# Output projection of a four-layer mixer trunk: weight blocks turned from 1024 rows by 256 columns to 512 by 512, with 512 columns per matmul

## Chip, core and metric

The kernel runs on one core of one Trainium2 chip. The metric is the device time of one execution in microseconds; a comparison uses the median of several. A difference below about 0.3% is treated as none.

## The reference

A sequence of 512 latent and 256 context tokens of width 1024 passes through four layers. Each layer normalises its input, scales and shifts it (a modulation computed from a conditioning vector), mixes the tokens, projects the mixed features back to width 1024 and adds the result to the residual stream:

```
h  = rmsnorm(x, g_pre[i]) * (1 + scale) + shift
y  = mixer(h, ...)                # the mixer's last step is: o @ w_out
x  = x + gate * rmsnorm(y, g_post[i])
```

The mixers are gated linear attention (layers 0 and 3), windowed attention (layer 1) and an RG-LRU recurrence (layer 2). `w_out` has 1024 rows in layers 0, 1 and 3 and 1280 rows in layer 2. In the last layer only the 512 latent tokens are projected.

## The kernel before, in words

**Products.** All large products are done in float32 precision by three passes: each operand is split into a high and a low float32r part, and `hi*hi + hi*lo + lo*hi` is accumulated in PSUM. So each chunk of 128 contraction rows costs three matmuls. Activations are held as `Rh` and `Rl`, features on the partitions, in 8 chunks of 128 features by 768 tokens.

**Weights.** `plan` (line 287) lists a layer's weight blocks in the order of use. A block has 1024 rows by 256 columns. `loadw` (line 221) loads it in two DMAs of 512 rows (512 KB each, tile `raw`, two buffers) on the SP queue; its `convert` splits each piece with `split` (line 242): ScalarE writes the high part (line 243), then VectorE, or for every third split GpSimd, writes the low part (line 246). The tiles `wh` and `wl` have two buffers each. `weights` (line 335) hands out the next block and first fetches and converts the one after it, so the conversion of a block waits until the block two before it has been read for the last time.

**The finish of a layer** (`finish`, line 733) opens six PSUM banks of 512 columns. It splits the mixer's output `OG` into `Rh` and `Rl` chunk by chunk (lines 750 and 751), finishes the modulation work that is still pending (`background`, line 753), loads the residual `x`, and then does the output projection for six token tiles of 128 tokens (four in the last layer), context tiles 4 and 5 first:

- Blocks o0 and o1 (the first two quarters of the columns): for each pair of token tiles one bank holds two results of 256 columns; `product` (line 761) issues 24 matmuls of 256 columns for a token tile (30 in layer 2, whose last two contraction chunks come from the tiles `exh`, `exl` and the weights `wxh`, `wxl`). `take` (line 773) then evacuates: ScalarE squares and sums (line 776), VectorE multiplies by the gate row `gpt` (line 777).
- Blocks o2 and o3 (the other two quarters) are both there before `halves` (line 811) runs: for each token tile it does the third quarter, later the fourth, into the two halves of one bank; after the fourth come `take` on 512 columns, `post` (line 781: sum of the three partial sums, then 1/rms on GpSimd, lines 589 and 590) and later `residual` (line 789).
- In layers 0 to 2 the second part is written out by hand (line 864 on; the order on TensorE, ScalarE and VectorE is the program's order). Between the products of `halves` it places what leads to the next layer's operand: `residual`, `square` (line 596), `scale` (line 796, y), then `norm` (transposes at line 613, ScalarE at 617, VectorE at 624 and 625) in four steps for each pair of tiles. In layers 0 and 1 each `step` also carries two matmul groups of a later layer's modulation (line 499, weights `rawp`, with transposes at line 517). The order around the first transposes is:

```
run(halves((2, 4), (2, 5), (3, 4), (3, 5)))
h = halves((2, 0), (2, 1), (3, 0), (3, 1))
...
next(h)            # quarter 2 of tile 0
...
next(h)            # quarter 2 of tile 1
scale(5)
step((4, 5), 0)    # transposes of tiles 4 and 5
```

- In the last layer (`final`, line 824) each token tile runs `halves((2, tt), (3, tt))` and then `residual`, in an order that the planner of the framework may still change by readiness.

After the last product, `begin` (line 401) and the next mixer's first products follow.

Of the kernel before, what the change touches and what calls it, by code (L numbers as in the profile page):

```python
# [10 lines left out]
F32 = mybir.dt.float32  # L11
# [8 lines left out]
P = 128  # L20
# [55 lines left out]
def body(ctx: ExitStack, tc: tile.TileContext, I, out, layers=(0, 1, 2, 3)):  # L76
# [28 lines left out]
    @contextmanager  # L105
    def phase(name, single=2, double=2):
        """a phase's own SBUF pool and the PSUM banks that phases share out anew, singly and in pairs"""
        with ExitStack() as st:
            if open_already:
                st.push(open_already.pop())  # L110
            else:
                open_banks(st, name, single, double)
            yield open_pool(st, name, bufs=1)

# [10 lines left out]
    # the first phase's banks are there from the start  # L125
# [26 lines left out]
    # the RG-LRU's small parameters  # L152
# [7 lines left out]
    def lru_parameters(bank):  # L160
# [10 lines left out]
        # half biases for the gates' tanh form of the sigmoid  # L171
        V.tensor_scalar(hb, ps[:, 50:90], 0.5, None, op0=ALU.mult)
        # softplus(-lam) = max(-lam, 0) + ln(1 + exp(-|lam|)), times -4 and 2
# [13 lines left out]
    class Mixed:  # L187
        """the mixer's output, features on the partitions; its last two chunks' room is free for
        other use until they are written"""
# [31 lines left out]
    def loadw(pieces):  # L221
        """256 columns; what is returned takes them apart once they are there"""
# [18 lines left out]

    def split(h, l, x):
# [5 lines left out]
    def load_g1(a):  # L248
        """the low-rank gate projection, both directions, four times over along the columns"""
# [19 lines left out]
    def load_g2(a, zero=True, load=True):  # L269
        """three times over, each direction's rows against its own columns; gpt is free for it"""  # L270
# [16 lines left out]
    def plan(i):  # L287
        """the layer's weight blocks in the order of use"""
# [31 lines left out]
        for n in range(4):  # L320
            yield f"o{n}", cols(wo[0 : KC * P], (n * 256, 256))
# [13 lines left out]
    def weights(key, ahead=True):  # L335
        """the next weight block, with the one after it on its way"""
# [7 lines left out]
    def passes(ps, a, b, kc):  # L344
        """ps += a^T b for pairs (hi, lo) of operand getters over the contraction chunks."""
# [8 lines left out]
    # products begun ahead of their use: the bank's part, and how many tokens of it are done  # L354
    begun = {}

    def ws_part(w, c0, ps, t0, n):
        """128 output columns on the partitions, tokens along the free axis"""
# [8 lines left out]
    def product_steps(ps, w, c0, t0, n):  # L367
        """the same, one product at a time; yields what each takes"""
# [9 lines left out]
    def ws(w, c0, stream):  # L378
        """128 output columns for all tokens of the stream"""
# [8 lines left out]
    def ws_ctx(w):  # L388
        """the context's tokens for both halves of the columns, in one bank but for what was begun elsewhere"""
# [11 lines left out]
    def begin(stream):  # L401
        """the first 256 tokens of what the next weight block brings first"""
# [11 lines left out]
    def ts(wk, kc, rk, tts, ps=None):  # L414
        """tokens on the partitions, 256 output columns along the free axis, for two token tiles."""
# [15 lines left out]
    def gate(pool, w, c0, stream, dst, parts=1):  # L431
        """dst (128 channels, the stream's tokens) *= silu(z), z a 128-column block of the projection."""
# [3 lines left out]
    def gate_ctx(pool, w, dst):  # L436
        """the same for both of the block's halves"""
        silu_times(pool, ws_ctx(w)[0], dst[:, :, CTX0:])
# [15 lines left out]
    def z_steps(pool, w, c, b, put, streams=("ctx", "lat")):  # L454
        """silu(z) for chunk b of the mixer's output, ahead of the output or behind it; put holds
        the token tiles of which either is there"""
# [48 lines left out]
    def mod_ss(i, n, bank, pool=None, bufs=1):  # L505
        """shift (n 0-3) and scale (n 4-7) of layer i, with the features on the partitions; in three steps."""
# [28 lines left out]
    def mod_gate(i, n, bank, pool=None, bufs=1):  # L535
        """gate * g_post of layer i, on all partitions; in three steps."""
# [34 lines left out]
    def background(n):  # L571
        """the next of the modulations; the last step of each comes with the one after it"""
# [20 lines left out]
    def unit_rstd(pool, x, xn):  # L593
        """1 / rms(x); xn is overwritten"""
# [4 lines left out]
    def unit(pool, x, xn):  # L599
        """xn = x / rms(x)"""  # L600
# [3 lines left out]
    def norm_part(pool, i, pr, xn, k, h=None):  # L604
        """xn: token tile -> x / rms(x); writes two chunks of h of layer i, transposed and split, to Rh / Rl."""
# [21 lines left out]
    def first_norm(i):  # L627
        """the same before the first layer, where the modulation comes late: x / rms(x) waits
        transposed in OG, and goes on as its chunks' shift and scale come in. A GLA's first
        products follow chunk by chunk."""  # L630
# [54 lines left out]
        # (two groups share a bank: the first one's first product clears the flags of both)  # L685
# [47 lines left out]
    def finish(i, kc, extra, last, final, xsrc, xdst):  # L733
        """out projection of OG, post norm, residual, and the next layer's pre norm."""
# [3 lines left out]
        with phase(f"fin{i}", 6, 0) as fp:  # L738
# [15 lines left out]
            for tt in tts_all:  # L754
# [3 lines left out]
                ssq[tt] = fp.tile([P, 3], F32, name=f"ssq{tt}")  # L758
            R = (Rh, Rl)

            def product(w, q, tt, ps, k0=0, k1=kc):
                """a quarter of the columns for a token tile"""
                cq = slice(q * 256, (q + 1) * 256)
                for k in range(k0, k1):
                    for u, v in ((0, 0), (0, 1), (1, 0)):
                        l = R[u][:, k, :] if k < KC else extra[u][:, k - KC, :]
                        r = w[v][:, k, :] if k < KC else wx[v][:, k - KC, cq]
# [5 lines left out]
            def take(q, tt, ps):  # L773
# [918 lines left out]
```

## Time and profile before

| | |
|---|---|
| times of three runs | 1570.82, 1573.35, 1574.89 us (median 1573.35) |
| span of the profiled execution, first to last instruction | 1568.0 us |
| time of the profiled execution itself | not listed; the three times above are 2.8 to 6.9 us over its span |
| TensorE busy with matmuls | 1489.2 us, 95% of the span |
| VectorE, ScalarE, GpSimd busy | 66%, 49%, 18% |
| matmuls | 12819 |
| mean granted TensorE clock | 0.988 of full speed |

The profile names an instruction by its line, its engine and `output<-inputs`. A matmul's listed duration is its passage through the array; since matmuls are pipelined, what counts is the distance between the starts of two neighbours, called pitch below. An idle time in brackets stands in front of the instruction that ended it, with what released it.

### The profile page before, as it was taken

The numbers are of one execution on the slowest core, as the hardware profiler recorded it, in microseconds if no ns is written. First come the engines' busy times: TensorE is split into PE (matmuls) and PEld (weight loads), VectorE is DVE, ScalarE is ACT, GpSimd is POOL, SyncE is SP. The second block draws the span as 40 slices with busy tenths as digits, with TensorE's granted clock in tenths as the row PEclk, the third lists the DMA queues.
The fourth block names the chain that finished last, engine by engine and source line by source line (L and its number), as shares of the span: only waits on it lengthen the run. The fifth ranks groups of instructions, "written<-read, shape, count | busy, mean of one in ns | idle before, by whom it ended". The sixth has DMA issues, their size and how long they took to land.

```text
span 1568.0 us, 31484 instructions
## 1 busy us (share of the span) xinstructions
PE 1489.2 (95%) x12819; PEld 1279.1 (82%) x12819; DVE 1040.6 (66%) x1918; ACT 774.9 (49%) x1567; POOL 289.1 (18%) x338
## 2 busy tenths in 40 slices
PE   6989999999999999999999999899999999999998
PEld 3777788889987777788789877778899877878888
DVE  5586647575363388787872679989852675776753
ACT  5644343534252376565552556666742545454241
POOL 2221302112121200101001212222311311211211
PEclk8999999999999999999999999999999999999999
DMA  9432324113474532222134633222151243112132
GB/s 306 139 114 78 122 62 132 55 47 130 158 235 133 165 83 58 61 59 55 54 115 143 224 102 114 67 64 61 57 176 44 99 143 98 38 53 68 45 108 81
DMA packets 153057, 162.51 MB, mean 104 GB/s; under 512 B 12418, under 2 KB 141968, under 8 KB 152912
## 3 DMA queue, kind: packets, MB, share of 16 engines
q1 hardware_dynamic: 147456, 146.56, 30.6%
q10 hardware_dynamic: 5456, 13.94, 2.5%
q8 instruction: 101, 1.65, 0.4%
q14 instruction: 44, 0.36, 0.1%
HBM read 138.44 MB, written 11.53 MB: 96 GB/s over the span
## 4 chain that ended last, share of the span: by engine, by line
PE 49%; DVE 12%; ACT 5%; issue 4%; DMA 3%; POOL 1%; SPq 1%; POOLq 0%; ACTq 0%; DVEq 0%
PE mxt L768 16%; PE pjt L372 9%; PE pjt L362 5%; PE pjt L349 3%; PE mxt L1464 3%; PE mxt L1450 2%; PE mxt L499 2%; PE sct L1563 2%; DMA raw<-in_w_mod_dram 1%; PE mxt L1146 1%; PE mxt L1412 1%; PE mxt L1395 1%; DVE wl L246 1%; ACT wh L243 1%; DMA bb<-in_b_mod_dram 1%
## 5 line engine op out<-in xcount | busy, mean ns | idle before, releaser
L362 PE MATMUL pjt<-Rh,wh 128*128 128x256 f32 (+1 forms) x592 | 199.6, 338 | 8.8 <-DVE Rh L624 5.3
L768 PE MATMUL mxt<-wh,Rh 128*128 128x256 f32 x704 | 200.7, 285 | 0.0
L362 PE MATMUL pjt<-Rl,wh 128*128 128x256 f32 (+1 forms) x592 | 198.8, 336 | 1.9 <-DVE Rl L625 1.6
L768 PE MATMUL mxt<-wh,Rl 128*128 128x256 f32 x704 | 198.9, 283 | 0.0
L768 PE MATMUL mxt<-wl,Rh 128*128 128x256 f32 x704 | 198.9, 283 | 0.0
L362 PE MATMUL pjt<-Rh,wl 128*128 128x256 f32 (+1 forms) x592 | 197.5, 334 | 0.0
L243 ACT CAST wh<-raw 128x1024 fp32r<-128x1024 f32 x118 | 122.8, 1050 | 88.6 <-PE pjt L362 22.4
L372 PE MATMUL pjt<-Rl,wh 128*128 128x512 f32 (+1 forms) x448 | 161.1, 360 | 0.0
L372 PE MATMUL pjt<-Rh,wh 128*128 128x512 f32 (+1 forms) x448 | 160.4, 358 | 0.0
L372 PE MATMUL pjt<-Rh,wl 128*128 128x512 f32 (+1 forms) x448 | 159.0, 355 | 0.0
L246 POOL TENSOR_TENSOR wl<-raw,wh 128x1024 fp32r<-128x1024 f32 x32 | 85.5, 2670 | 304.0 <-ACT wh L243 232.6
L768 PEld LDWEIGHTS mxt<-wh,Rh 128*128 128x128 f32 x704 | 134.9, 192 | 1.9 <-issue 1.6
L768 PEld LDWEIGHTS mxt<-wh,Rl 128*128 128x128 f32 x704 | 134.7, 192 | 0.3 <-DVE Rl L751 0.2
L768 PEld LDWEIGHTS mxt<-wl,Rh 128*128 128x128 f32 x704 | 134.9, 192 | 0.1
L362 PEld LDWEIGHTS pjt<-Rh,wh 128*128 128x128 f32 x592 | 112.7, 191 | 24.5 <-DVE Rh L624 6.9
L246 DVE TENSOR_TENSOR wl<-raw,wh 128x1024 fp32r<-128x1024 f32 x86 | 110.4, 1289 | 33.1 <-ACT wh L243 32.8
L362 PEld LDWEIGHTS pjt<-Rl,wh 128*128 128x128 f32 x592 | 112.7, 191 | 16.4 <-DVE Rl L625 4.0
L349 PE MATMUL pjt<-wh,Rh 128*128 128x256 f32 x432 | 124.2, 287 | 0.0
L349 PE MATMUL pjt<-wl,Rh 128*128 128x256 f32 x432 | 123.9, 287 | 0.0
L349 PE MATMUL pjt<-wh,Rl 128*128 128x256 f32 x432 | 123.8, 286 | 0.0
L362 PEld LDWEIGHTS pjt<-Rh,wl 128*128 128x128 f32 x592 | 112.9, 191 | 13.0 <-issue 1.2
L777 DVE TENSOR_TENSOR y<-mxt,gpt 128x256 f32<-128x256 f32 (+1 forms) x66 | 33.6, 512 | 110.8 <-ACT y L776 110.8
(293 smaller groups left out, 3673.9 us busy)
## 6 DMA issues: line engine op xcount, KB each, us to landing
rawp<-in_w_mod_dram SPq DMA_DIRECT2D x48, 512.0 KB, 6.2
raw<-in_w_mod_dram SPq DMA_DIRECT2D x48, 512.0 KB, 3.6
raw<-in_a_w_in_dram SPq DMA_DIRECT2D x32, 512.0 KB, 3.5
raw<-in_b_w_in_dram SPq DMA_DIRECT2D x20, 512.0 KB, 4.6
raw<-in_c_w_in_dram SPq DMA_DIRECT2D x20, 512.0 KB, 3.6
xd<-x SPq DMA_DIRECT2D x18, 512.0 KB, 2.6
raw<-in_a_w_out_dram SPq DMA_DIRECT2D x16, 512.0 KB, 3.4
x<-xd ACTq DMA_DIRECT2D x16, 512.0 KB, 8.8
```

Of the source, the lines that this page charges most:

```text
L243: S.copy(h, x)
L246: e.tensor_tensor(l, x, h.bitcast(F32), op=ALU.subtract)
L349: PE.matmul(ps, a(u, k), b(v, k), start=(n == 0), stop=(n == 3 * kc - 1))
L362: PE.matmul(ps, w[u][:, k, c0 : c0 + P], R[v][:, k, t0 : t0 + n], start=(k == 0 and u + v == 0), stop=(k == KC - 1 and u == 1),)
L372: PE.matmul(ps, w[u][:, k, c0 : c0 + P], R[x][:, k, t0 : t0 + n], start=(k == 0 and u + x == 0), stop=(k == KC - 1 and u == 1),)
L499: PE.matmul(ps[32 * g : 32 * g + 32, 0:256], sT[:, k, :], r2[k // 4][:, k % 4, :], start=(k < 4), stop=(k >= 4), skip_group_check=True,)
L768: PE.matmul(ps, l[:, tt * P : (tt + 1) * P], r, start=(k == 0 and u + v == 0), stop=(k == kc - 1 and u == 1),)
L777: V.tensor_tensor(y[tt][:, cq], ps, gpt[:, 1 if tt >= 4 else 0, cq], op=ALU.mult)
L1146: PE.matmul(ps[:, n, :], l, r, start=(m == 0), stop=(m == len(tm) - 1))
L1450: PE.transpose(u[e][:, c * P : (c + 1) * P], ps[e][:, m * P : (m + 1) * P], ident)
L1464: PE.matmul(po[64 * e : 64 * e + 64, 0:P], v[:, t, 64 * kv : 64 * kv + 64], pt[:, e, m * P : (m + 1) * P], start=(m == 0), stop=(m == len( ...
L1563: PE.matmul(ps[:, t0 : t0 + nn], wg[a][:, n, :], x[c][:, p0 : p0 + nn], start=(q == 0), stop=(q == 2),)
```

## The change

`plan` lists four blocks o0 to o3 by halves of the rows and halves of the columns; a block's two `raw` pieces are now two column quarters of one row half. The first two blocks are both row halves of the first 512 columns: six banks, one for each token tile, are opened in the first block and closed in the second. `halves` does the same per token tile for the other 512 columns. A matmul now has 512 columns. The 256 extra rows of layer 2 are added in the second row half. The hand-written order is otherwise the same. (Docstrings and comments that the diff also removes are left out here.)

```diff
+    def load_half(wo, kh, ch):
+        rs = []
+        for m in range(2):
+            r = raw()
+            c0 = ch * 512 + m * 256
+            nc.sync.dma_start(
+                r, wo[kh * 512 : (kh + 1) * 512, c0 : c0 + 256].rearrange("(k p) n -> p k n", p=P)
+            )
+            rs.append(r)
+
+        def convert():
+            w = [wp.tile([P, KC, 256], F32R, name=n, tag=n) for n in ("wh", "wl")]
+            wh, wl = (x.rearrange("p k n -> p (k n)").rearrange("p (k n) -> p k n", n=512) for x in w)
+            for m, r in enumerate(rs):
+                c = slice(m * 256, (m + 1) * 256)
+                split(wh[:, :, c], wl[:, :, c], r)
+            return wh, wl
+        return convert
...
         for n in range(4):
-            yield f"o{n}", cols(wo[0 : KC * P], (n * 256, 256))
+            yield f"o{n}", lambda n=n: load_half(wo, n % 2, n // 2)
...
-                ssq[tt] = fp.tile([P, 3], F32, name=f"ssq{tt}")
+                ssq[tt] = fp.tile([P, 2], F32, name=f"ssq{tt}")
...
-            def product(w, q, tt, ps, k0=0, k1=kc):
-                cq = slice(q * 256, (q + 1) * 256)
-                for k in range(k0, k1):
+            def product(w, kh, ch, tt, ps):
+                ks = list(range(4 * kh, 4 * kh + 4)) + (list(range(KC, kc)) if kh else [])
+                for k in ks:
                     for u, v in ((0, 0), (0, 1), (1, 0)):
                         l = R[u][:, k, :] if k < KC else extra[u][:, k - KC, :]
-                        r = w[v][:, k, :] if k < KC else wx[v][:, k - KC, cq]
+                        r = w[v][:, k % 4, :] if k < KC else wx[v][:, k - KC, ch * 512 : (ch + 1) * 512]
                         PE.matmul(
                             ps, l[:, tt * P : (tt + 1) * P], r,
                             start=(k == 0 and u + v == 0), stop=(k == kc - 1 and u == 1),
                         )
...
-            def take(q, tt, ps):
-                cq = slice(q * 256, (q + 1) * 256) if q < 2 else slice(512, 1024)
-                S.activation(y[tt][:, cq], ps, AF.Square, accum_out=ssq[tt][:, q : q + 1])
-                V.tensor_tensor(y[tt][:, cq], ps, gpt[:, 1 if tt >= 4 else 0, cq], op=ALU.mult)
+            def take(ch, tt, ps):
+                c = slice(ch * 512, (ch + 1) * 512)
+                S.activation(y[tt][:, c], ps, AF.Square, accum_out=ssq[tt][:, ch : ch + 1])
+                V.tensor_tensor(y[tt][:, c], ps, gpt[:, 1 if tt >= 4 else 0, c], op=ALU.mult)
...
-            for q in range(2):
-                w = weights(f"o{q}")
-                for pr in pairs:
-                    ps = mxt().rearrange("p (c n) -> p c n", c=2)
-                    for m, tt in enumerate(pr):
-                        product(w, q, tt, ps[:, m, :])
-                    for m, tt in enumerate(pr):
-                        take(q, tt, ps[:, m, :])
+            banks = {}
+            for kh in range(2):
+                w = weights(f"o{kh}")
+                for tt in tts_all:
+                    if not kh:
+                        banks[tt] = mxt()
+                    product(w, kh, 0, tt, banks[tt])
+                    if kh:
+                        take(0, tt, banks[tt])
             keep_pool.append(1)
             w = [weights("o2")]
             w.append(weights("o3", False))
...
             def halves(*parts):
                 ps = {}
-                for q, tt in parts:
+                for kh, tt in parts:
                     if tt not in ps:
                         ps[tt] = mxt()
-                    c = (q - 2) * 256
-                    product(w[q - 2], q, tt, ps[tt][:, c : c + 256])
+                    product(w[kh], kh, 1, tt, ps[tt])
                     yield
-                    if q == 3:
-                        take(2, tt, ps[tt])
+                    if kh:
+                        take(1, tt, ps[tt])
                         post(tt)
 
             if final:
                 for tt in tts_all:
-                    run(halves((2, tt), (3, tt)))
+                    run(halves((0, tt), (1, tt)))
                     residual(tt, 2 if tt == tts_all[-1] else 1)
...
-                run(halves((2, 4), (2, 5), (3, 4), (3, 5)))
-                h = halves((2, 0), (2, 1), (3, 0), (3, 1))
+                run(halves((0, 4), (0, 5), (1, 4), (1, 5)))
+                h = halves((0, 0), (0, 1), (1, 0), (1, 1))
...
-                h = halves((2, 2), (2, 3), (3, 2), (3, 3))
+                h = halves((0, 2), (0, 3), (1, 2), (1, 3))
```

## Rows read from the trace of the kernel before

**Rows 1.** The page: busy times, and the span in 40 slices.

```profile
PE 1489.2 (95%) x12819; PEld 1279.1 (82%) x12819; DVE 1040.6 (66%) x1918; ACT 774.9 (49%) x1567; POOL 289.1 (18%) x338
...
PE   6989999999999999999999999899999999999998
```

**Rows 2.** The page: the chain that ended last, by line.

```profile
PE mxt L768 16%; PE pjt L372 9%; PE pjt L362 5%; PE pjt L349 3%; PE mxt L1464 3%; PE mxt L1450 2%; PE mxt L499 2%; PE sct L1563 2%; DMA raw<-in_w_mod_dram 1%; PE mxt L1146 1%; PE mxt L1412 1%; PE mxt L1395 1%; DVE wl L246 1%; ACT wh L243 1%; DMA bb<-in_b_mod_dram 1%
```

**Rows 3.** Groups by line and shape, TensorE: one of three passes each.

```profile
L768 PE MATMUL mxt<-wh,Rh 128*128 128x256 f32 x704 | 200.7, 285 | 0.0
...
L768 PE MATMUL mxt<-wxl,exh 128*128 128x256 f32 x48 | 13.6, 285 | 0.3 <-POOL wxl L246 0.3
```

**Rows 4.** Stretches: length, PE, PEld, DVE, ACT, POOL busy (instructions), PEclk, DMA share, GB/s.

```profile
376.00:426.00 50.00, 50.00 (x417) 49.71 (x419) 17.58 (x31) 15.42 (x43) 9.89 (x6) 1.00 0.52 179
426.00:458.00 32.00, 32.00 (x317) 26.90 (x314) 18.55 (x39) 15.84 (x34) 6.63 (x14) 1.00 0.79 260
...
1203.00:1233.00 30.00, 29.60 (x250) 29.37 (x249) 16.46 (x29) 14.13 (x30) 7.62 (x16) 1.00 0.24 88
```

**Rows 5.** The chain in order of time (start, length): products of layer 0.

```profile
377.00 48.95 PE mxt L768 x408
```

**Rows 6.** Timeline of TensorE before layer 2's finish: matmuls of 512 columns (start, duration).

```profile
1130.90 0.39 PE L362 MATMUL pjt<-Rh,wh 128*128 128x512 f32 x1
...
1134.75 0.39 PE L362 MATMUL pjt<-Rh,wl 128*128 128x512 f32 x1
1136.13 0.50 PE L362 MATMUL pjt<-Rh,wh 128*128 128x512 f32 x1 [0.99 <-DVE gz L448]
1136.47 0.40 PE L362 MATMUL pjt<-Rl,wh 128*128 128x512 f32 x1
...
1138.11 0.39 PE L362 MATMUL pjt<-Rh,wl 128*128 128x512 f32 x1
```

**Rows 7.** Timelines of ScalarE, VectorE, TensorE in layer 2: from tile 5's product to its transposes.

```profile
1200.57 0.60 ACT L776 ACTIVATE y<-mxt 128x512 f32<-128x512 f32 x1 [2.91 <-PE mxt L768]
...
1207.44 0.75 DVE L796 TENSOR_SCALAR y<-x,rx 128x1024 f32<-128x1024 f32 x1 [0.72 <-POOL rx L590]
...
1207.58 0.27 PE L613 MATMUL mxt<-ident,y 128*128 128x128 f32 x1
1208.25 0.55 PE L613 MATMUL mxt<-ident,y 128*128 128x128 f32 x3 [0.40 <-DVE y L796]
```

**Rows 8.** Timeline of VectorE and TensorE in layer 0: the same place.

```profile
429.98 0.75 DVE L796 TENSOR_SCALAR y<-x,rx 128x1024 f32<-128x1024 f32 x1 [0.72 <-POOL rx L590]
...
431.16 0.66 PE L613 MATMUL mxt<-ident,y 128*128 128x128 f32 x4
```

**Rows 9.** Timelines of ScalarE and VectorE in layer 3: the conversion of block o3.

```profile
1537.90 0.39 ACT L776 ACTIVATE y<-mxt 128x256 f32<-128x256 f32 x1 [4.32 <-PE mxt L768]
...
1539.58 1.05 ACT L243 CAST wh<-raw 128x1024 fp32r<-128x1024 f32 x1
...
1540.82 1.22 DVE L246 TENSOR_TENSOR wl<-raw,wh 128x1024 fp32r<-128x1024 f32 x1
```

**Rows 10.** Timelines of ScalarE, VectorE and SP in layer 0: two conversions, and two loads behind them.

```profile
450.68 2.00 ACT L243 CAST wh<-raw 128x1024 fp32r<-128x1024 f32 x2
...
452.13 2.36 DVE L246 TENSOR_TENSOR wl<-raw,wh 128x1024 fp32r<-128x1024 f32 x2
...
453.38 1.51 SPq L227 DMA_DIRECT2D raw<-in_b_w_in_dram  x2
...
457.70 1.05 ACT L243 CAST wh<-raw 128x1024 fp32r<-128x1024 f32 x1 [1.26 <-PE mxt L768]
```

**Rows 11.** Timelines of VectorE and GpSimd at the end of layer 0's finish.

```profile
461.64 1.27 DVE L789 SCALAR_TENSOR_TENSOR x<-y,ry,x 128x1024 f32<-128x1024 f32 x1
...
463.90 3.41 DVE L789 SCALAR_TENSOR_TENSOR x<-y,ry,x 128x1024 f32<-128x1024 f32 x1
...
463.63 2.60 POOL L246 TENSOR_TENSOR wl<-raw,wh 128x1024 fp32r<-128x1024 f32 x1
```

## The prediction

> **What bounds the kernel now.** I read the page first: TensorE is busy for 95% of the span, and in 36 of the 40 slices it stands at nine tenths or more [rows 1]. Busy is not the same as fast, so the second view is the chain that ended last: the product line of the output projection, L768, is its largest entry with 16% [rows 2]. Third, the groups by shape: L768 has 3 passes of 704 matmuls and 3 of 48 for layer 2's extra rows, 2256 matmuls of 256 columns, and almost no idle time in front of them; the one wait is 0.3 us for `wxl` [rows 3]. Fourth, the stretches: in layer 0 the engine has no idle time from 376 to 458 us, VectorE and ScalarE have at least four tenths of their time free beside it, the DMA share is 0.52 and then 0.79, and the granted clock is 1.00, the level of 2.4 GHz; in layer 2 the second part loses 0.40 us of 30 [rows 4]. So in the stages that the change touches TensorE sets the time, by the pitch of its matmuls.
>
> **The pitch.** In layer 0's run the chain has 408 matmuls of 256 columns in 48.95 us, 0.1200 us each [rows 5]. For 512 columns I need another line: in the projection just ahead of layer 2's finish the starts from 1130.90 to 1134.75 us stand 17 pitches apart, 0.2265 us each [rows 6]. Columns at 2.4 GHz take 0.1067 and 0.2133 us, so both carry about 13 ns that does not grow with the columns. That is what the change removes once for every pair.
>
> **The change, part by part.**
>
> 1. *Matmuls.* 2256 x 0.1200 = 270.7 us become 1128 x 0.2265 = 255.5 us: **-15.2 us**. All of it lies on TensorE's own path [rows 4].
>
> 2. *Run starts.* A 512-column run starts slower: after a pause, seven pitches from 1136.47 to 1138.11 us take 1.64 us, 0.055 us more than seven settled ones [rows 6]. In the second part of a finish products stand between transposes, so there are some 24 new starts in all: 0 (the 256-column runs may pay the same) to 1.3 us. I take the middle, **+0.7 us**.
>
> 3. *Layer 2's first transposes.* Here the change adds a wait. TensorE's order is fixed by hand: between the last product of tile 5 and the transposes of tiles 4 and 5 stand two products, tile 0's and tile 1's. They were 30 matmuls each, 7.20 us. Now the row half that comes first has 12 matmuls of 512, 2.72 us, and the extra rows wait for the second half: 5.44 us. The work they cover does not shrink: it runs from tile 5's `take` at 1200.57 us over 1/rms, `residual`, `square` and `scale` (y ready at 1208.19), and the transposes behind it already waited 0.40 us [rows 7]. So the wait grows by 7.20 - 5.44 = 1.76 us. Queued behind it on TensorE are all later products of that finish, so it counts in full: **+1.8 us**. Bounds: 0, if the chain ran faster, which nothing in it suggests, to 1.8.
>
> 4. *The same place in layers 0 and 1.* There each product shrinks only from 2.88 to 2.72 us, and modulation matmuls stand between. In layer 0 y is ready at 430.73 us and the transposes start at 431.16 [rows 8]: 0.43 us of room, of which two products take 0.32. **0**; without the modulation matmuls it would cost what part 3 costs.
>
> 5. *Layer 2's extra weights.* They are needed only in the second row half, so the 0.3 us wait goes [rows 3]: **-0.3 us**. What is late next there is nothing up to the second half, some 16 us further on.
>
> 6. *Block o3.* Its conversion must wait for the last read of o1. A matmul over 512 columns needs both converted pieces from its first column on, where before the first four chunks needed only one. In layer 3 the second-half product follows the first after one product, now 2.72 us. Before, the last low part ended at 1542.04 us, 4.1 us after the last-but-one `take` began [rows 9]. Now: a `take` of 0.60 us [rows 7], 1.45 us until the low parts start and 2.36 us for both [rows 10], 4.4 us, against some 2.8 us until the first matmul that reads `wl`. If TensorE stands still for that, 1.6 us. The planner orders this part by readiness and may put tile 1's first half in between; then 0. The nearest row is layer 2's late `wxl`, where other products filled all but 0.3 us [rows 3], so I take **+0.4 us**. In layers 0 to 2 two products stand in front (5.4 us): no wait.
>
> 7. *Evacuation.* Six banks stay open over two blocks; in each layer twelve `take`s of 256 columns become six of 512. All lie beside products and ScalarE and VectorE have that much time free [rows 4]. The number of banks handed out before the hand-written part is six, as before, so its rotation stays. The first half's `take`s come later, in the second block, 2.72 us apart (4.08 in layer 2) against 0.60 us of work. **0**; if that cover went, one `take` per layer, under 1 us.
>
> 8. *Loads and splits.* The same pieces of 512 rows by 256 columns on the same SP queue, in another order; nothing is moved past another load. The count of splits is equal, so every third still goes to GpSimd. In layers 0 and 1 the second part asks the DMAs for the same bytes in slightly less time: share 0.79 becomes about 0.82. **0**.
>
> 9. *Tail.* In layer 0 the next layer's weights are loaded from 453.38 us, behind two conversions, and split at 457.70 us, just after the last product released a buffer [rows 10]. Three products shorter by 0.16 us each bring TensorE's end 0.5 us nearer to that load. 0 to 0.5 us in each of layers 0 and 1; I take **+0.2 us** together.
>
> Sum: -15.2 + 0.7 + 1.8 - 0.3 + 0.4 + 0.2 = **-12.4 us**. The profiled execution is known by its span, 1568.0 us; its own time is not listed, and the three times lie 2.8 to 6.9 us above that span. I set the sum against the span (1555.6) and carry it to the median: 1573.35 - 12.4 = **1561.0 us**, 0.8% less. A measurement of this kernel can tell about 0.3% (4.7 us) from no change.
>
> **A rule to weigh.** The 13 ns for each matmul are the whole gain. The Trainium skill (TensorE: Matmul & The Clock Gate, section Back-to-back issue gap) gives another size: its table has 262 cycles for 256 columns and 518 for 512, a constant of about 2.5 ns. By it the pairs would save 1128 x 2.5 ns = 2.8 us, and part 1 would be cancelled by the waits. The trace does not agree: 0.1200 us is 13 ns over the columns' time, not 2.5.
>
> **Rivals.**
>
> - *The chain beside TensorE sets the second part.* If VectorE, ScalarE and GpSimd decide there, only the first two blocks (half the matmuls) and layer 3 gain: some 7.6 + 1.3 us less parts 2, 3, 6 and 9, about -6 us, 1567 us. For it: the wait in [rows 7]. Against: no idle time from 426 to 458 us [rows 4]. Chance 0.15.
> - *Better cover.* The first block needs only chunks 0 to 3, so its products could slip into gaps at the end of the mixer, such as the 0.99 us of [rows 6], and parts 2, 6 and 9 might cost nothing: -15.2 + 1.8 - 0.3 - 1.0 = -14.7 us, and -16.5 if part 3 were covered too: about 1558 us. Chance 0.12.
> - *The constant does not halve.* If the 13 ns belong to the columns in these products (weights as moving operand, which no 512-column row shows), the pitch is 0.240 us, part 1 is 0, and the rest leaves +2.8 us: 1576 us, no change; if products of 12 never leave the starting pitch of 0.234 us [rows 6], part 1 is -6.4 and the sum without part 2 -4.3: 1569 us. Chance 0.03.
> - *A constant of 2.5 ns*, as that page has it: a pitch of 0.2375 us in these products, between the two just priced; -2.8 us and waits of 2.8 us cancel: 1573 us, no change. The 408 matmuls of [rows 5] speak against it. Chance 0.02.
> - *Slower: GpSimd beside VectorE.* In layer 0's tail one `residual` took 3.41 us instead of 1.27 beside a low part on GpSimd that ran for 2.60 us [rows 11]: 2.1 us on the path to the next layer. An earlier finish shifts the two against each other. It decides only from eight more such meetings (12.4 + 4.7 = 17.1 us): 1578 us. Three tails hardly have room for them. Chance 0.06.
>
> That the change does not do what it says would need matmuls that stay at 256 columns; 512-column float32r matmuls run as single instructions elsewhere [rows 6], so I give it nothing of its own.
>
> **How the numbers follow.** The forecast has 0.62. Its own ends: parts 2, 6 and 9 at their upper bounds give -15.2 + 1.3 + 1.8 - 0.3 + 1.6 + 1.0 = -9.8, 1563.5 us; all at 0 give -13.7, 1559.6 us. The range takes in the better cover (1557, and 1 us for the spread of the runs) and the first rival (1567 and 1 us): 1556 to 1568 us. Outside lie the last three rivals and the edges, under 2 in 10. Faster: 0.62 + 0.12 + two thirds of the first rival, 0.84. Same: its rest and the two cases of the constant, 0.10. Slower: 0.06.
>
> **What would show it.** L768 with 1128 matmuls of 512 columns at a pitch near 0.227 us, `x204` in about 46.3 us where 408 stood in 48.95; about 2.2 us of idle time before layer 2's first L613 transposes; none in front of layer 0's; L768 in layer 3 waiting for `wl` by 0 to 1.6 us; `wxl` no longer a releaser. A pitch of 0.23 or more, or new idle time above 3 us in the finishes, would make the prediction wrong.

## The result, and the profile after

The changed kernel takes 1563.27 us (median of six runs, 1561.32 to 1566.23), the kernel before on the same chip 1572.09 us; the ratio is 0.9943 with a 95% interval of 0.9924 to 0.9961, so some 9.0 us less. Among the six runs of the kernel before is one of 5019.49 us, which the ratio leaves out; without it their median is 1570.82 us and the difference of the medians 7.5 us. The forecast was 1561.0 us, 12.4 us less, with a range of 1556 to 1568. The profiled execution took 1563.12 us with a span of 1561.3, against 1568.0 before: 6.6 us less (from the unrounded spans). So the direction and the range hold, but at least a quarter of the forecast gain is missing, and the trace shows it missing in one layer.

The page's busy times, and then the groups by line and shape on TensorE, of the changed kernel (L768 has become L789, the transposes L613 are L634):

```profile
PE 1479.5 (95%) x11691; PEld 1223.2 (78%) x11691; DVE 1036.3 (66%) x1896; ACT 770.9 (49%) x1523; POOL 286.0 (18%) x338
```

```profile
L789 PE MATMUL mxt<-wh,Rh 128*128 128x512 f32 x352 | 140.2, 401 | 3.2 <-ACT wh L264 3.2
...
L789 PE MATMUL mxt<-wl,Rh 128*128 128x512 f32 x352 | 138.1, 392 | 0.2 <-POOL wl L267 0.2
L634 PE MATMUL mxt<-ident,y 128*128 128x128 f32 x144 | 22.6, 297 | 2.4 <-DVE y L816 2.4
...
L789 PE MATMUL mxt<-wxl,exh 128*128 128x512 f32 x24 | 9.3, 390 | 0.0
```

The matmuls fell from 12819 to 11691 [rows 1], by the 1128 pairs. Where [rows 3] had three passes of 704 there are three of 352, all of 512 columns, and the wait for `wxl` is gone. One idle time is new and one has grown: 3.2 us in front of a product with a high weight part, released by ScalarE's conversion, and 2.4 us in front of the transposes, where the kernel before had 0.9 (0.40 of them those of [rows 7]). The first was in no part of the forecast. Together that is 4.7 us of new idle time in the finishes; the prediction had named more than 3 us as a sign that it is wrong.

The chain in order of time (start, length) has a run of layer 0's products (the 144 of its first two blocks and the 60 that follow them) and the products of layer 3:

```profile
377.45 46.24 PE mxt L789 x204
...
1510.56 43.78 PE mxt L789 x192
```

46.24 us stand where [rows 5] had 48.95: the first 204 starts of that run are 0.2267 us apart. By stage, from the first to the last start of a product line:

| stage | before, us | after, us | change |
|---|---|---|---|
| layer 0's finish | 80.55 | 77.04 | -3.51 |
| layer 1's finish | 80.55 | 77.10 | -3.45 |
| layer 2's finish | 90.07 | 93.13 | **+3.06** |
| layer 3's finish | 46.21 | 43.54 | -2.67 |

Three layers gave what was forecast. Layer 2 was forecast at about -3.1 us and became slower by as much. Here is layer 2's finish in stretches (length; busy time of PE, PEld, DVE, ACT, POOL with instructions; granted clock PEclk; DMA share; GB/s):

```profile
1134.29:1150.39 16.10, 16.10 (x73) 13.34 (x71) 9.31 (x12) 5.36 (x10) 2.56 (x1) 1.00 0.66 246
1150.39:1158.00 7.61, 4.24 (x11) 2.59 (x10) 1.23 (x1) 2.78 (x3) 2.38 (x1) 0.78 0.34 109
1158.00:1199.00 41.00, 41.00 (x182) 33.98 (x181) 12.86 (x16) 9.89 (x23) 3.23 (x5) 1.00 0.22 67
1199.00:1206.00 7.00, 5.07 (x17) 3.72 (x17) 2.63 (x4) 2.13 (x4) 1.34 (x3) 0.76 0.18 76
1206.00:1230.00 24.00, 24.00 (x125) 20.18 (x124) 13.15 (x24) 12.41 (x27) 5.68 (x11) 1.00 0.19 67
```

Three stretches are full and have the clock at 1.00. In the two others TensorE idles for a part, and the mean granted clock of the stretch is 0.78 and 0.76. The first of them on TensorE's timeline (start, duration as listed):

```profile
1150.39 0.39 PE L789 MATMUL mxt<-wh,Rl 128*128 128x512 f32 x1
1153.98 2.35 PE L789 MATMUL mxt<-wh,Rh 128*128 128x512 f32 x5 [3.20 <-ACT wh L264]
1156.49 0.80 PE L789 MATMUL mxt<-wl,Rh 128*128 128x512 f32 x1 [0.17 <-POOL wl L267]
1157.08 0.63 PE L789 MATMUL mxt<-wh,Rl 128*128 128x512 f32 x1
1157.51 0.44 PE L789 MATMUL mxt<-wh,Rh 128*128 128x512 f32 x1
1157.79 0.39 PE L789 MATMUL mxt<-wl,Rh 128*128 128x512 f32 x1
```

The first block's 72 products end, and block o1 is not converted: 3.59 us between two starts, 3.36 more than a pitch. The next eight pitches take 3.81 us instead of 1.81; most are 0.427 us, the time of 512 columns at the 1.2 GHz level, and in one of them stands a second short wait, for `wl` (0.17 us as listed). So the wait is paid twice: 3.4 us of idling and 2.0 us behind it, most of it slow matmuls, 5.4 us together. Now the same engine at the first transposes:

```profile
1199.27 0.39 PE L789 MATMUL mxt<-wh,Rl 128*128 128x512 f32 x1
1200.45 0.33 PE L634 MATMUL mxt<-ident,y 128*128 128x128 f32 x1 [0.80 <-DVE y L816]
1201.92 0.89 PE L634 MATMUL mxt<-ident,y 128*128 128x128 f32 x3 [1.14 <-DVE y L816]
1202.45 0.78 PE L789 MATMUL mxt<-wh,Rh 128*128 128x512 f32 x1
1203.03 0.63 PE L789 MATMUL mxt<-wl,Rh 128*128 128x512 f32 x1
1203.46 0.63 PE L789 MATMUL mxt<-wh,Rl 128*128 128x512 f32 x1
```

This is the wait that part 3 foresaw, in place of the 0.40 us of [rows 7]; behind it the pitch is 0.427 us again.

Why is o1 late? The timelines of SP, ScalarE and GpSimd of the changed kernel, then of ScalarE, GpSimd and TensorE before:

```profile
1143.15 16.86 SPq L248 DMA_DIRECT2D raw<-in_c_w_out_dram  x5
...
1151.54 1.04 ACT L264 CAST wh<-raw 128x1024 fp32r<-128x1024 f32 x1 [10.10 <-DMA raw<-in_c_w_out_dram]
1152.88 1.04 ACT L264 CAST wh<-raw 128x1024 fp32r<-128x1024 f32 x1 [0.30 <-DMA raw<-in_c_w_out_dram]
...
1154.06 2.38 POOL L267 TENSOR_TENSOR wl<-raw,wh 128x1024 fp32r<-128x1024 f32 x1 [10.93 <-ACT wh L264]
```

```profile
1159.14 1.05 ACT L243 CAST wh<-raw 128x1024 fp32r<-128x1024 f32 x1 [10.29 <-DMA raw<-in_c_w_out_dram]
...
1161.72 2.40 POOL L246 TENSOR_TENSOR wl<-raw,wh 128x1024 fp32r<-128x1024 f32 x1 [11.18 <-ACT wh L243]
...
1164.37 0.28 PE L768 MATMUL mxt<-wh,Rh 128*128 128x256 f32 x1
```

Counted from the first product (1134.29 and 1141.75), o1's first cast starts at 17.3 us after and at 17.4 before, and its last low part ends at 22.2 and 22.4 us. Nothing became later. The need became earlier: before, o1 was first read 180 matmuls of 256 columns in, at 22.6 us, 0.25 us after its last low part; now it is read after 72 matmuls of 512, at 16.3 us.

### The profile page after: what moved, and what is told of

Same layout as the page of the kernel before. It is cut to its first block, busy times and chain, and to the rows that moved or that the text cites. A ratio compares the mean times of both kernels' runs of the same rounds, so it can differ in the third digit from the quotient of the medians.

```text
span 1561.3 us, 29167 instructions
## 1 busy us (share of the span) xinstructions
PE 1479.5 (95%) x11691; PEld 1223.2 (78%) x11691; DVE 1036.3 (66%) x1896; ACT 770.9 (49%) x1523; POOL 286.0 (18%) x338
## 4 chain that ended last, share of the span: by engine, by line
PE 50%; DVE 11%; ACT 6%; DMA 3%; issue 3%; POOL 2%; SPq 1%; ACTq 0%; POOLq 0%; DVEq 0%
PE mxt L789 14%; PE pjt L393 10%; PE pjt L383 7%; PE pjt L370 4%; PE mxt L1484 3%; PE sct L1583 2%; PE mxt L1470 2%; PE mxt L520 2%; PE mxt L1166 1%; PE mxt L1432 1%; DMA raw<-in_w_mod_dram 1%; ACT wh L264 1%; PE mxt L1415 1%; DVE ls L985 1%; DMA bb<-in_b_mod_dram 1%
## 5 line engine op out<-in xcount | busy, mean ns | idle before, releaser
L789 PE MATMUL mxt<-wh,Rh 128*128 128x512 f32 x352 | 140.2, 401 | 3.2 <-ACT wh L264 3.2
L789 PE MATMUL mxt<-wl,Rh 128*128 128x512 f32 x352 | 138.1, 392 | 0.2 <-POOL wl L267 0.2
L789 PE MATMUL mxt<-wh,Rl 128*128 128x512 f32 x352 | 138.1, 392 | 0.0
L383 PEld LDWEIGHTS pjt<-Rh,wh 128*128 128x128 f32 x592 | 113.2, 192 | 21.9 <-DVE Rh L645 6.7
L383 PEld LDWEIGHTS pjt<-Rl,wh 128*128 128x128 f32 x592 | 113.3, 192 | 16.5 <-DVE Rl L646 4.4
L383 PEld LDWEIGHTS pjt<-Rh,wl 128*128 128x128 f32 x592 | 113.4, 192 | 12.7 <-issue 1.2
L393 PEld LDWEIGHTS pjt<-Rh,wh 128*128 128x128 f32 x448 | 84.7, 189 | 11.7 <-issue 3.6
L393 PEld LDWEIGHTS pjt<-Rh,wl 128*128 128x128 f32 x448 | 84.8, 189 | 10.8 <-issue 3.2
L393 PEld LDWEIGHTS pjt<-Rl,wh 128*128 128x128 f32 x448 | 84.8, 189 | 10.5 <-issue 2.8
L1451 ACT ACTIVATE pe<-mxt,mxs 128x256 f32<-128x256 f32 (+2 forms) x128 | 70.5, 555 | 32.0 <-DVE mxs L1443 27.9
```

The costliest lines, as they stand in the source:

```text
L383: PE.matmul(ps, w[u][:, k, c0 : c0 + P], R[v][:, k, t0 : t0 + n], start=(k == 0 and u + v == 0), stop=(k == KC - 1 and u == 1),)
L393: PE.matmul(ps, w[u][:, k, c0 : c0 + P], R[x][:, k, t0 : t0 + n], start=(k == 0 and u + x == 0), stop=(k == KC - 1 and u == 1),)
L789: PE.matmul(ps, l[:, tt * P : (tt + 1) * P], r, start=(k == 0 and u + v == 0), stop=(k == kc - 1 and u == 1),)
L1451: S.activation(p[:, o : o + w], u[e][:, :w], AF.Exp, bias=nm, scale=0.125, accum_out=den[:, n : n + 1],)
```

## The experiments

The theory: layer 2 loses its gain by two waits, o1's conversion and y in front of the transposes, and each costs more than its idle time because the granted clock falls behind it. The rivals: 512-column products are slow there by themselves; the chain beside TensorE sets that layer, so that a wait taken away turns up elsewhere; the loss comes from the layers before. Each kernel changes layer 2 only.

### Extra rows between the two row halves

```diff
+            rows = [list(range(0, 4)), list(range(4, KC))]
+            more = list(range(KC, kc))
...
+                if kh and more:
+                    for tt in tts_all:
+                        product(None, more, -1, 0, tt, banks[tt])
...
-                    product(w, kh, 0, tt, banks[tt])
+                    product(w, rows[kh], KC - 1, 0, tt, banks[tt])
```

> Only layer 2 differs from the changed kernel: for the first 512 columns the 36 matmuls of the extra rows stand between the two row halves instead of in the second. Theory: block o1's conversion is late there because its raw pieces share two buffers with the extra rows, and each wait costs twice, since the granted clock falls behind it (pitch 0.427 instead of 0.2265 us). The 36 matmuls are 8.2 us of cover, against a wait of 3.6 us: the wait on wh goes, and the clock stays at 1.00 in that stretch; layer 2's run of products shrinks from 93.1 to about 87.5 us (waits of 3.6 and 0.8 and some 10 matmuls with 0.2 us too much), the kernel from 1563.3 to about 1557.5; the 2.6 us in front of the first transposes stay. Rival (512-column products of layer 2 are slow by themselves, whatever waits): the pitch stays at 0.427 in the same place and the run of products shrinks by the wait of 3.6 us alone or less, to 89.5 us or more. Rival (the landing of o1 is pushed out by whatever stands ahead): the wait moves with it, 92 to 93 us.

Measured: 1555.11 us, ratio to the kernel before 0.9911 (0.9884 to 0.9938); layer 2's finish 87.79 us. The only wait left there, by the list of TensorE's waits (total, times, longest), is the one at the transposes:

```profile
PE mxt L634 <- DVE y L818: 1.9, 2, 1.1
```

The first 180 products take 40.80 us, which is 180 pitches of 0.2267, where the changed kernel needed 46.16. So the slow matmuls were not a property of 512 columns in this place: without the wait they are gone too, 5.36 us for a wait of 3.4.

### Extra rows first in the second part

```diff
-                    product(w[kh], kh, 1, tt, ps[tt])
+                    product(w[kh], rows[kh] + ([] if kh else more), KC - 1, 1, tt, ps[tt])
```

> Only layer 2's second part differs from the changed kernel: the extra rows go into a tile's first half product, which has 18 matmuls, and the second half 12. Theory: the transposes of tiles 4 and 5 wait because only 24 matmuls (5.44 us) cover 1/rms, residual, square and scale; with 36 matmuls (8.15 us) for the 7.65 us that the chain took, the 2.6 us of waits there go, and with them the fall of the clock behind: layer 2's run of products shrinks from 93.1 to about 89.5 us, the kernel to about 1559.7; the wait of 3.6 us for o1's conversion stays. Rival (the chain beside TensorE sets the second part, whatever stands between): the wait turns up at a later place and the run of products stays at 92.5 us or more.

Measured: 1560.62 us, 0.9938 (0.9913 to 0.9962); layer 2's finish 89.86 us. Its waits:

```profile
PE mxt L791 <- ACT wh L264: 3.1, 1, 3.1
PE mxt L791 <- POOL wl L267: 1.1, 1, 1.1
```

The transposes wait for nothing, and the second part takes 42.94 us instead of 46.97: 4.03 us for idle times of 1.9. The wait did not come back at a later place, so the chain over VectorE, ScalarE and GpSimd does not set the second part once 36 matmuls cover it. The wait for o1 stays, as expected.

### Both

The two edits together.

> Both of the two edits: extra rows between the row halves for the first 512 columns, and in the first half product for the second 512. Theory: both waits and both falls of the clock go, the gains add: layer 2's run of products about 84 us (from 93.1), the kernel about 1554 us, ratio to the kernel before about 0.988. Rival (chain or loads set layer 2, TensorE only waits elsewhere): less than 6 us of the 9 come, 1557.5 us or more.

Measured: 1554.94 us, 0.9902 (0.9880 to 0.9925); layer 2's finish 83.74 us. The row of stretches over that finish (PE busy, as above):

```profile
1131.00:1216.00 85.00, 85.00 (x388) 70.42 (x387) 38.56 (x56) 30.31 (x62) 13.47 (x18) 1.00 0.33 111
```

85 us without a gap, at a clock of 1.00. The gains add: 40.80 and 42.94 us for the two parts.

### Layer 2 as before, the others as after

The four blocks of layer 2 go back to 1024 rows by 256 columns, with the products and evacuations of the kernel before:

```diff
+            if kind == 2:
+                yield f"o{n}", cols(wo[0 : KC * P], (n * 256, 256))
+            else:
+                yield f"o{n}", lambda n=n: load_half(wo, n % 2, n // 2)
```

> Layer 2's output projection as in the kernel before (blocks of 1024 rows by 256 columns, 256 columns per matmul), layers 0, 1 and 3 as in the changed kernel. Theory: the three layers keep their gains of 3.5, 3.5 and 2.7 us, each of them on its own, and layer 2 is back at 90.1 us: 3 us faster than the changed kernel, about 1560.3 us. Rival (the loss in layer 2 comes from the earlier finish of the layers before it, not from its own blocks): layer 2 stays near 93 us and the time at 1563.

Measured: 1561.50 us, 0.9941 (0.9919 to 0.9963); layer 2's finish is back at 90.10 us, and the others keep 77.04, 77.05 and 43.55. So the loss belongs to layer 2's own blocks, and the rival falls. The 3 us do not show in the median: it is 1.2 above the expected value, and inside the spread. The trace of this kernel has its loss elsewhere: from the last product of layer 2 to the first of layer 3, where its program is the same as the changed kernel's, it took 288.3 us at a mean granted clock of 0.96, and the changed kernel 283.0 us at 0.98.

### Own buffers for the raw pieces of the extra rows

```diff
-                    r = raw()
+                    r = y[2 + k].rearrange("p (k n) -> p k n", k=4)
```

(with the y tiles of two token tiles allocated ahead of it)

> As the changed kernel, but the raw pieces of layer 2's extra rows lie in two tiles that are free at that time (those of y for two token tiles) and not in the two raw buffers that block o1 needs. Theory: o1's loads were held until the extra rows were split, were issued at 1143.2 and 1144.2 us and landed 8 us later behind the six loads of x; with buffers of their own they are issued some 10 us or more earlier, o1 is converted before it is needed at the end of the first 72 matmuls, and the wait of 3.6 us and the fall of the clock go: layer 2's run of products 87.5 us, the kernel 1557.5 us. Rival (the conversion is late because ScalarE and VectorE are busy until then, or because wh and wl of the block two before are still read): the loads land earlier, the wait stays, 93 us.

Measured: 1558.49 us, 0.9929 (0.9911 to 0.9947); layer 2's finish 87.07 us. Timelines of SP, ScalarE and TensorE:

```profile
1120.41 19.00 SPq L248 DMA_DIRECT2D raw<-in_c_w_out_dram  x3
...
1131.60 2.01 ACT L264 CAST wh<-raw 128x1024 fp32r<-128x1024 f32 x2
...
1145.17 1.05 ACT L264 CAST wxh<-y 128x1024 fp32r<-128x1024 f32 x1 [10.84 <-DMA y<-in_c_w_out_dram]
...
1189.68 0.39 PE L793 MATMUL mxt<-wh,Rl 128*128 128x512 f32 x1
1190.86 0.33 PE L634 MATMUL mxt<-ident,y 128*128 128x128 f32 x1 [0.79 <-DVE y L820]
1192.33 0.55 PE L634 MATMUL mxt<-ident,y 128*128 128x128 f32 x3 [1.14 <-DVE y L820]
1192.63 0.48 PE L793 MATMUL mxt<-wh,Rh 128*128 128x512 f32 x1
1192.94 0.40 PE L793 MATMUL mxt<-wl,Rh 128*128 128x512 f32 x1
1193.18 0.39 PE L793 MATMUL mxt<-wh,Rl 128*128 128x512 f32 x1
```

o1 is converted at 1131.60 us, 2.5 us after the first product instead of 17.3, and the wait is gone. It was the shared pair of buffers that held its loads until the extra rows were split. The lateness moved on to the extra rows themselves, which are now cast from 1145.17 us; that costs 0.9 us (first part 41.74 us). The last six rows hold a surprise: the wait at the transposes is the same as in the changed kernel, but behind it the clock does not fall. The pitch is 0.23 to 0.31 us at once, and the second part takes 45.33 us where the changed kernel needed 46.97. The two differ by the slow matmuls alone, 1.6 us.

### Dummy matmuls in the wait

```diff
+                if kc > KC:
+                    idle = pjt()
+                    for n in range(9):
+                        PE.matmul(idle, Rh[:, 0, 0:P], w[0][0][:, 0, :], start=(n == 0), stop=(n == 8))
```

> As the changed kernel, with 9 matmuls of 512 columns whose result nobody reads, placed in front of the first transposes of layer 2: work added, no wait taken away. Theory (the clock falls behind an idle TensorE): 9 x 0.2265 = 2.0 us fill most of the 2.6 us of waits; y is ready at the same time, but the clock stays at its upper level, and the matmuls behind the transposes have a pitch of 0.2265 instead of 0.427 us: layer 2's run of products 1 to 1.5 us shorter although 9 matmuls were added. Rival (the slow matmuls behind the transposes have another cause, such as their weight loads or PSUM banks): the same slow matmuls, run of products not shorter.

Measured: 1563.50 us, 0.9957 (0.9943 to 0.9972). TensorE's timeline at the transposes:

```profile
1201.56 2.21 PE L898 MATMUL pjt<-wh,Rh 128*128 128x512 f32 x9
1203.60 0.93 PE L634 MATMUL mxt<-ident,y 128*128 128x128 f32 x4
1204.28 0.47 PE L789 MATMUL mxt<-wh,Rh 128*128 128x512 f32 x1
1204.60 0.39 PE L789 MATMUL mxt<-wl,Rh 128*128 128x512 f32 x1
1204.83 0.39 PE L789 MATMUL mxt<-wh,Rl 128*128 128x512 f32 x1
```

Nine useless matmuls made the second part shorter, 45.32 us against 46.97, because the products behind the transposes run at 0.23 us. That is 1.65 us, a little over the 1 to 1.5 us that the theory named; weight loads and banks are as they were, so that rival falls. That the useless matmuls kept the clock up is not shown by this one trace, since the kernel with own raw buffers had no fall behind the same wait without them. The whole finish is only 0.2 us shorter, since the wait for o1, which this kernel leaves alone, cost 6.8 us here (first part 47.59 us) instead of 5.4.

### Later loads of x

```diff
-                nc.scalar.dma_start(xs[tt], xsrc(tt))
+                if kc == KC:
+                    nc.scalar.dma_start(xs[tt], xsrc(tt))
...
+                if kh and kc > KC:
+                    for tt in tts_all:
+                        nc.scalar.dma_start(xs[tt], xsrc(tt))
```

> As the changed kernel, but layer 2's six loads of x (512 KB each, ScalarE's queue) are issued behind the first block's products and not ahead of them; the raw buffers are shared as before. It splits the lateness of o1 into its two parts: the late issue (after the extra rows' splits) and the landing 8 us later. Theory: the 8 us are the x loads that were issued up to 4 us earlier; without them the two pieces of o1 land in 3.4 us like the extra rows' pieces, some 4 us earlier, which is more than the wait of 3.6 us: the run of products of layer 2 shrinks from 93.1 to about 88 us. Rival (the late issue alone decides, the landing is slow for another reason): the wait stays within 1 us of 3.6 and the run of products above 92 us.

Measured: 1562.72 us, 0.9938 (0.9918 to 0.9957); layer 2's finish 89.86 us. The planner moved three of the six loads ahead again, so only the other three came later. Timelines of ScalarE, GpSimd and TensorE:

```profile
1150.41 1.05 ACT L264 CAST wh<-raw 128x1024 fp32r<-128x1024 f32 x1 [6.40 <-DMA raw<-in_c_w_out_dram]
...
1152.95 2.35 POOL L267 TENSOR_TENSOR wl<-raw,wh 128x1024 fp32r<-128x1024 f32 x1 [7.26 <-ACT wh L264]
...
1155.36 0.50 PE L790 MATMUL mxt<-wl,Rh 128*128 128x512 f32 x1 [1.79 <-POOL wl L267]
```

o1's first cast comes 4.7 us after the issue of its load (1145.72 us) instead of 8.4 us (1143.15 to 1151.54), 13.6 us after the first product instead of 17.3. So the loads of x ahead of it do slow its landing: with all six ahead, as in nine of the traces here, the same stretch is 7.8 to 8.9 us. The wait shrank only to 1.95 us, though, since it is now GpSimd's low part of the second piece that comes last. Neither the 88 nor the 92 us of the expectation: the late issue and the slow landing both have a share.

### The changed kernel and both edits once more

> The changed kernel once more, beside the version with both edits on the same chip: its ratio to the kernel before is expected at 0.994 to 0.996, with waits of 3.6 and 2.6 us in layer 2.

> Both edits once more, beside the changed kernel on the same chip. Theory: 9 us less in layer 2, so a ratio to the changed kernel of about 0.994, to the kernel before of 0.989; run of products of layer 2 within 0.5 us of 83.7. Rival (the gain is given back later, since the spread of the earlier medians hid it): the medians differ by less than 4 us though layer 2 is 9 us shorter.

Measured on one chip: 1562.76 us (0.9946, interval 0.9927 to 0.9966) and, with both edits, 1556.89 us (0.9904, 0.9886 to 0.9922). Layer 2's finish took 94.61 and 83.74 us. The medians differ by 5.9 us, the intervals do not overlap, and the layer is 10.9 us shorter: neither the full gain nor the rival's "less than 4". What became of the rest is not settled. In the two profiled executions the three stretches ahead of layer 2's finish that lie outside the output projection, and that the edits leave as they are, were 1.6, 1.9 and 1.5 us longer with both edits. Between layer 2 and layer 3, where all these programs are the same, the traces have 281.5 to 288.3 us without a relation to the edits: the two traces of this one version have 282.40 and 287.21.

Layer 2's finish in all kernels, first 512 columns and second, us:

| kernel | first | second | whole |
|---|---|---|---|
| before | 44.22 | 45.85 | 90.07 |
| changed, and once more | 46.16, 47.60 | 46.97, 47.01 | 93.13, 94.61 |
| extra rows between | 40.80 | 46.99 | 87.79 |
| extra rows first in part two | 46.92 | 42.94 | 89.86 |
| both, and once more | 40.80, 40.80 | 42.94, 42.94 | 83.74, 83.74 |
| own raw buffers | 41.74 | 45.33 | 87.07 |
| dummies | 47.59 | 45.32 | 92.91 |
| layer 2 as before | 44.26 | 45.84 | 90.10 |
| later loads of x | 42.89 | 46.97 | 89.86 |

## Why the prediction was right, and where it was not

- **Matmuls (part 1)** were right in size: 0.2267 us is the pitch, and 144 products of layer 0's first part take 32.64 us, where 288 x 0.1200 = 34.56 stood. The constant of 13 ns is paid once per instruction and did halve. The rule of the Trainium skill that was weighed there (TensorE: Matmul & The Clock Gate, section Back-to-back issue gap), with 2.5 ns, which the page gives for an isolated matmul, is not what this kernel shows.
- **Run starts (part 2)**: layers 0, 1 and 3 gained 3.51, 3.45 and 2.67 us where the pitches alone give 3.89, 3.89 and 2.59 (576 x 0.1200 - 288 x 0.2265, and two thirds of it): 0.7 us lost, as taken for the whole kernel. It lies where the step put it: in layers 0 and 1 the pitches between products exceed the settled one by 0.90 and 0.96 us in all, where it was 0.52 before; in layer 3 by 0.25 in both kernels.
- **Layer 2's transposes (part 3)** were right in mechanism: the cover, the place and the idle time, about 2.4 us (45.33 us with the wait and no slow matmuls, 42.94 without either) against 2.2 forecast. The size was wrong, because the step priced idling alone: 46.97 - 42.94 = 4.0 us, 1.6 of them slow matmuls. The fall of the clock behind a pause stood in the trace of before, in a projection of layer 2's mixer, and was not read. TensorE's timeline there:

```profile
1025.58 0.50 PE L362 MATMUL pjt<-Rh,wh 128*128 128x512 f32 x1 [2.42 <-ACT up L1512]
1025.91 0.40 PE L362 MATMUL pjt<-Rl,wh 128*128 128x512 f32 x1
1026.15 0.40 PE L362 MATMUL pjt<-Rh,wl 128*128 128x512 f32 x1
1026.38 0.48 PE L362 MATMUL pjt<-Rh,wh 128*128 128x512 f32 x1
...
1027.08 0.63 PE L362 MATMUL pjt<-Rh,wl 128*128 128x512 f32 x1
1027.51 0.63 PE L362 MATMUL pjt<-Rh,wh 128*128 128x512 f32 x1
1027.94 0.63 PE L362 MATMUL pjt<-Rl,wh 128*128 128x512 f32 x1
```

  Behind 2.42 us of idling the first four pitches are still 0.23 to 0.33 us, and the next seven 0.43; the mean granted clock from 1025.58 to 1030.03 us is 0.62. The Trainium skill (TensorE: Matmul & The Clock Gate, section HAM oscillation — how this bites in real kernels) describes a kernel in which TensorE's waits for transfers bring the clock down, so that work starts slow behind each; the traces here agree for most waits, with 0.427 us instead of 0.2265, but not for all, and here the fall can come some matmuls after the restart.
- **The same place in layers 0 and 1 (part 4)**: no wait, as forecast.
- **Layer 2's extra weights (part 5)** is the step that failed. The wait for `wxl` went, but the step's "what is late next there is nothing up to the second half, some 16 us further on" was false: at those 16 us o1 itself is first read, 6.3 us earlier than before, and its conversion had had 0.25 us to spare. The step followed the weights that moved back in the order and not the block that moved forward. Cost: 5.4 us in the profiled execution, 5.4 to 6.8 in the four traces that leave the order up to o1 as it was (changed, its repetition, extra rows first in part two, dummies).
- **Block o3 (part 6)**: the planner put a part of tile 1's first half in between in layer 3 (the first `take` of the second part comes after 30 matmuls and not after 24), and 43.54 us is within 0.3 us of 191 pitches; 0 was right and 0.4 too much. **Evacuation and loads (parts 7 and 8)** cost nothing in layers 0, 1 and 3; in layer 2 o1's loads stood behind the extra rows' pieces and beside the loads of x, as before, and what had been just in time was now late. **The tail (part 9)**, 0.2 us, is below what the stretches between layers vary by.

Summed for layer 2: forecast -3.1 us (360 x 0.2265 - 720 x 0.1200 = -4.9, a third of part 2, and parts 3 and 5), measured +3.1, a miss of 6.2. o1 is 5.4 of it, the transposes beyond the forecast 1.8 (4.0, less the 0.4 of before and the 1.8 of part 3). That is 1.0 too much, and most of it stands in the version without waits: its 83.74 us are 6.3 less than before, where the pitches and the two old waits of 0.4 and 0.3 give 5.6. The forecast held within its range because three layers of four carried it, and because the kernel before measured 1572.09 us and not the 1573.35 us that it started from. As a gain, 9.0 us lies outside the forecast's own ends of 9.8 and 13.7 us, and inside the range only by the room that was left for another rival, the chain beside TensorE, which the extra rows first in the second part refute. That a miss of 6.2 us in one layer stayed inside is luck. The chance of 0.06 for "slower" had no such mechanism in it.

A version that beats both kernels came out of this: with both edits 1554.94 and 1556.89 us, 0.990 of the kernel before.

## What to carry to other kernels

When a loop order changes, list for every operand the time of its first read before and after, counted from the stage's start, and set it against the time at which it is ready; an operand without an idle time in front of it may still have only a quarter of a microsecond to spare. Price a wait of TensorE at its idle time and up to nearly as much again for the matmuls behind it (3.4 and 2.0 us here, 3.7 and 3.1 in the repetition, 2.4 and nothing with own raw buffers). Where some rows of a sum are ready early and others late, their order inside the accumulation is free: moving 36 matmuls was worth 5.3 us in layer 2, more than the 4.9 us of halving its 720.

## What the runs showed of the hardware

The fall of the clock behind a wait is not certain. Behind the same wait at the transposes (idle times of about 0.8 and 1.1 us) the pitch was 0.427 us in the changed kernel, in its repetition, with the extra rows between and with the later loads, and 0.23 to 0.31 us with own raw buffers; behind the 1.8 us for GpSimd in the kernel with the later loads it did not fall either. What decides is left open. Nor does it always come at once: with the extra rows between, and in the repetition, the first four pitches behind the transposes were still 0.23 to 0.34 us. And the first load of o1, 512 KB, took 8.4 us from its issue to the cast with six loads of x issued up to 4.4 us ahead of it, and 4.7 us with three.
